# A two-layer decoder trunk on one core: earlier weight sums, a queue order, residual rows in place, a norm by column halves

## The chip, the cores and the metric

The kernel runs on one core of a Trainium2 chip. The metric is the device time of one execution in microseconds (us). The kernel before has a median of 1347.66 us over 3 runs (1346.14 to 1349.74).

## What is computed

The reference is a trunk of two post-norm layers on 512 tokens of width 1024, in float32:

```python
for l in range(DEPTH):                                   # DEPTH = 2
    proj = x @ w_in[l]
    ...
    o_a = hgrn2_mixer(hq, hf, hi, hg, lbs[l], hg_norm_w[l])      # gated linear recurrence
    o_b = nsa_mixer(nq, kc, vc, ks, vs, kw, vw, gt, ...)         # sparse attention
    mix = jnp.concatenate([o_a, o_b], axis=-1) @ w_out[l]
    x = layer_norm(ALPHA * x + mix, ln1_g[l], ln1_b[l])
    ffn = (jax.nn.silu(x @ w_ffn_gate[l]) * (x @ w_ffn_up[l])) @ w_ffn_down[l]
    x = layer_norm(ALPHA * x + ffn, ln2_g[l], ln2_b[l])
```

## The kernel before

Every product of float32 matrices is made of three TensorE matmuls on two parts: a weight or activation tile `raw` is split into a rounded part `h` (a ScalarE copy) and a rest `raw - h` (a VectorE subtraction), and `mm3` (L82 to L84) sums high x high, low x high and high x low. So each product needs one ScalarE and one VectorE instruction of its weight tile before it can run. PE is TensorE, ACT ScalarE, DVE VectorE, POOL GpSimd, SP SyncE.

A layer runs as one stream of stages, the same for both layers (times of layer 0, and of layer 1 in brackets): projections, recurrence and attention (0 to about 282 us; about 690 to 948); the out-projection with its norm, in a first half (`first_half`, contraction over the attention's first rows, 512 columns at a time) and a second half (`second_half` and the loop behind it, by quarters q of the columns), then `norm_turn` for two blocks of 256 tokens (282 to 345; 948 to 1015); gate and up (345 to 553; 1015 to 1223); the down projection (553 to 690; 1223 to 1344); the final norm.

**Gate and up** use Strassen's seven products on 2x2 blocks. `stage` loads what one unit needs: two raw tiles `a` and `d` and two sums `s1`, `s3`, each a load by SP into which POOL then issues a second DMA that adds (`accum_op`, L104 and L105). There are 20 units of seven products. `norm_rest` (L753 to L757) is the part of the norm that is left over for the residual: POOL loads the gain and shift rows, broadcast to all partitions, as one 1 MB tile `lnp` (L704), and DVE multiplies and adds on four row tiles `r`. It is hooked to a unit of this stage by number.

**Down** (`first` to `fourth`, then the loop over q with the products Q, M and N) is a Strassen scheme too. For each q = 0 to 3 a running sum of weight blocks is kept in one tile: a load, an adding DMA, split and product (`first`), a second adding DMA, split and product (`third`), a third adding DMA, split and product (`fourth`). The sums of q = 0, 1, 2 lie in the ring "f" of three buffers, that of q = 3 in `ws`. The loop behind it makes one more sum of two blocks for each q, `s3`, by a load into "f" and one adding DMA; product Q uses it. The last `fourth`, of q = 3, comes behind the products Q and M of q = 0.

What sets the order is a scheduler: it simulates the program with its own durations and gives each engine a fixed list, which the engine then works through in order. So a wait on any engine holds up all that is listed behind it, and an edit in one place reorders others. DMAs are issued by SP (plain loads) and by POOL (adding DMAs, `lnp`, and the residual loads `xr`), each in the order of its list. The weights' ring "f" is also used by `xr` (L886), by the weights of quarter 2 of the out-projection's second half (L902) and by the tile `xr2` of `norm_turn`.

Of the kernel before, what the change touches and what calls it, by code (L numbers as in the profile page):

```python
# [34 lines left out]
class Kern:  # L35
# [58 lines left out]
    def stage(self, sa, sb):  # L94

        nc = self.nc
        with self.tc.high_priority(offset=3000):
            self.turn += 1
            tag, bufs = ("wr", 2) if self.turn % 3 else ("pt", 2) if self.turn == 3 else ("f", 3)
            a = self.sb.tile([128, 1024], F32, name="wraw", tag=tag, bufs=bufs)  # L100
            s1, s3, d = (self.sb.tile([128, 512], F32, name=n, tag=t, bufs=2) for n, t in (("ws1", "st"), ("ws3", "pc"), ("wd", "wd")))
            nc.sync.dma_start(s1, sb[:, 512:])
            nc.sync.dma_start(s3, sa[:, :512])
            nc.gpsimd.dma_start(s1, sb[:, :512], accum_op=OP.add)  # L104
            nc.gpsimd.dma_start(s3, sb[:, :512], accum_op=OP.add)  # L105
            nc.sync.dma_start(a, sa)
            nc.sync.dma_start(d, sb[:, 512:])
        return a, s1, s3, d
# [619 lines left out]
    def norm_turn(self, l, which, b, rows, x, raw=None):  # L728


        nc = self.nc
        for t in (2 * b, 2 * b + 1):
            mean, rs = self.norm_stats(t)
            nb = self.small(1, "nb", tag="l")
            nc.vector.tensor_scalar(nb, mean, rs, -1.0, op0=OP.mult, op1=OP.mult)
            nc.scalar.activation(rows[t], rows[t], AF.Identity, scale=rs, bias=nb)
        for k2 in range(0, NK, 2):
            pt = self.ps("t")
            p3 = pt.rearrange("p (k t) -> p k t", t=256)
            tmp = raw(b, k2) if raw else self.m([128, 2, 256], "xt")  # L740
            for i in range(2):
                k = k2 + i
                for j in range(2):
                    nc.tensor.transpose(p3[:, i, j * 128:(j + 1) * 128], rows[2 * b + j][:, k * 128:(k + 1) * 128], self.ident)
                nc.scalar.activation(tmp[:, i], p3[:, i], AF.Identity, scale=self.lnt[:, l, 2 * which, k:k + 1],
                                     bias=self.lnt[:, l, 2 * which + 1, k:k + 1])
            xh, xl = (a[k2 // 4][:, k2 % 4:k2 % 4 + 2, b * 256:(b + 1) * 256] for a in x)
            nc.scalar.copy(xh, tmp)
            nc.vector.tensor_tensor(xl, tmp, xh.bitcast(F32), op=OP.subtract)
# [12 lines left out]
    def layer(self, l):  # L762
# [95 lines left out]
        def rblocks():  # L858
            R.extend(self.big("r") for _ in range(2))
            rows.extend(R[t // 2].rearrange("p a b -> p (a b)")[:, (t % 2) * 1024:(t % 2 + 1) * 1024] for t in range(NT))  # L860

        def quart(b, q):
# [13 lines left out]
        def first_half(c):  # L876

            def f():
                ws = [self.load_w(io["wo1"][l, c, i]) for i in range(2)]
                cs = slice(c * 512, (c + 1) * 512)  # L880
                for b in range(2):
                    pts = {t: self.ps("d") for t in (2 * b, 2 * b + 1)}
                    for i in range(2):
                        self.wide_mm(pts, ws[i], ysf, i, i == 0, i == 1)
                    xr = self.sb.tile([128, 2, 512], F32, name="xr", tag="f", bufs=3)
                    for e, (t, p) in enumerate(pts.items()):  # L886
                        nc.gpsimd.dma_start(xr[:, e], self.xres[t * 128:(t + 1) * 128, cs])
                        nc.vector.scalar_tensor_tensor(rows[t][:, cs], xr[:, e], ALPHA, p, op0=OP.mult, op1=OP.add)
            return f
# [95 lines left out]
        def up(j):  # L985
            tmp = {}

            def take(part, acc, add):
                r, c = (int(x) - 1 for x in part)
                g = hidden(j + r)  # L990
                with tc.high_priority(offset=4000):
# [14 lines left out]
        self.seven([(io[w][l, j], io[w][l, j + 1], f(j)) for j in range(2, NF, 2) for w, f in (("wg", gate), ("wu", up))], R,  # L1006
                   {3: lambda: self.norm_rest(l, 0, rows, None)})

# [24 lines left out]

        def raw_w(src, plus=None, tag=("wr", 2)):
            t = self.sb.tile([128, 1024], F32, name="wraw", tag=tag[0], bufs=tag[1])
            nc.sync.dma_start(t, src)
            if plus is not None:
                nc.gpsimd.dma_start(t, plus, accum_op=OP.add)
            return t
# [13 lines left out]
        def first(q):  # L1053

            with tc.high_priority(offset=3000):
                if q < 3:
                    s = raw_w(wd[1, 2 * q], wd[1, 2 * q + 1], ("f", 3))
                else:
                    s = self.big("ws").rearrange("p a b -> p (a b)")[:, :1024]
                    nc.sync.dma_start(s, wd[1, 2 * q])  # L1060
                    nc.gpsimd.dma_start(s, wd[1, 2 * q + 1], accum_op=OP.add)
            r11, r12, _, r22 = half[q]
# [10 lines left out]
            with tc.high_priority(offset=3000):  # L1073
                nc.gpsimd.dma_start(s, wd[0, 2 * q], accum_op=OP.add)

# [5 lines left out]
        def third(q):  # L1081
# [4 lines left out]
            with tc.high_priority(offset=3000):  # L1086
                nc.gpsimd.dma_start(sums[q], wd[0, 2 * q + 1], accum_op=OP.add)

# [34 lines left out]
        for q in range(QS):  # L1123
# [3 lines left out]
            with tc.high_priority(offset=3000):  # L1127
                s3 = raw_w(wd[0, i], wd[1, i], ("f", 3))
                p12, p22 = raw_w(wd[0, i + 1]), raw_w(wd[1, i + 1])
# [162 lines left out]
```

## Time and profile before

| what | value |
|---|---|
| median of 3 runs | 1347.66 us (1346.14 to 1349.74) |
| the profiled execution, own time | 1353.65 us |
| its span, first to last instruction | 1351.9 us |
| mean granted TensorE clock | 0.989 |
| PE, DVE, ACT, POOL busy | 97%, 75%, 55%, 14% of the span |
| DMA moved | 186.54 MB, mean 138 GB/s |

The profiled execution is 6.0 us above the median; every time in the text is from it, counted from the span's start. PE is busy nearly all the time, so what can be won or lost lies in its idle moments, some 40 us in all (the span less its busy time), and in the stretches in which its clock was granted at half.

### The profile page before, as it was taken

What the parts mean: (1) busy time and instruction counts of PE and PEld (TensorE: products, weight loads), DVE (VectorE), ACT (ScalarE), POOL (GpSimd) and SP (SyncE); (2) the same over time, 40 slices, a digit from 0 to 9 for tenths busy, and PEclk for the clock granted to TensorE, in tenths of its full rate; (3) what the DMA queues carried; (4) which work ended last, traced back from release to release, by engine and by line L of the source; (5) the groups of instructions that cost most, each with busy time, mean ns of one, the idle gap of its engine ahead of it and who ended that gap; (6) DMA issues with size and microseconds to landing.
All of it is one profiled execution on the core that took longest, in us unless ns stands there. A gap on an engine that the chain in (4) does not pass through costs nothing.

```text
span 1351.9 us, 23468 instructions
## 1 busy us (share of the span) xinstructions
PE 1311.2 (97%) x8853; PEld 1200.4 (89%) x8853; DVE 1012.4 (75%) x2021; ACT 749.6 (55%) x1495; POOL 192.5 (14%) x275
## 2 busy tenths in 40 slices
PE   8999999999999999999999999999999999999997
PEld 6988999789999999877899989987899999997776
DVE  4755798866887778967667668988559877788767
ACT  5254777844655555645452558777256555556530
POOL 1140111111011121110011100111010111111102
PEclk9999999999999999999999999999999999999999
DMA  7253212252467778586433221132515777866852
GB/s 236 79 164 102 79 56 74 84 161 76 149 167 185 189 189 197 136 223 174 152 140 116 73 92 63 63 102 71 166 29 179 178 184 180 215 158 150 213 196 79
DMA packets 67682, 186.54 MB, mean 138 GB/s; under 512 B 8175, under 2 KB 8351, under 8 KB 67056
## 3 DMA queue, kind: packets, MB, share of 16 engines
q1 hardware_dynamic: 44640, 124.73, 27.9%
q0 software_dynamic: 21920, 58.47, 21.2%
q10 hardware_dynamic: 1008, 1.84, 0.4%
q8 instruction: 69, 1.13, 0.3%
q14 instruction: 45, 0.37, 0.1%
HBM read 180.76 MB, written 7.10 MB: 139 GB/s over the span
## 4 chain that ended last, share of the span: by engine, by line
PE 59%; DVE 5%; DMA 5%; ACT 2%; issue 2%; POOL 0%; POOLq 0%; DVEq 0%; ACTq 0%
PE ps_d L83 10%; PE ps_d L82 10%; PE ps_d L84 10%; PE ps_t L84 3%; PE ps_t L82 3%; PE ps_t L83 3%; DMA wraw<-in_wd 3%; PE ps_s L82 2%; PE ps_s L83 2%; PE ps_s L84 2%; DMA ws<-in_wd 1%; PE ps_t L647 1%; DVE wlo L1019 1%; DVE hop L1019 1%; PE ps_h L390 1%
## 5 line engine op out<-in xcount | busy, mean ns | idle before, releaser
L116 ACT CAST whi<-wraw 128x512 fp32r<-128x512 f32 x160 | 98.6, 620 | 123.1 <-PE ps_d L83 93.3
L82 PE MATMUL ps_d<-xh,whi 128*128 128x256 f32 (+1 forms) x424 | 141.9, 338 | 2.0 <-ACT gates L497 1.2
L84 PE MATMUL ps_d<-xh,wlo 128*128 128x256 f32 (+1 forms) x424 | 142.6, 337 | 0.0
L83 PE MATMUL ps_d<-xl,whi 128*128 128x256 f32 (+1 forms) x424 | 141.7, 335 | 0.6 <-DVE mv L712 0.6
L117 DVE TENSOR_TENSOR wlo<-wraw,whi 128x512 fp32r<-128x512 f32 x160 | 108.9, 687 | 44.5 <-ACT whi L116 42.1
L84 PE MATMUL ps_d<-th,wlo 128*128 128x256 f32 x480 | 133.7, 284 | 2.4 <-DVE wlo L117 2.4
L83 PE MATMUL ps_d<-tl,whi 128*128 128x256 f32 x480 | 134.9, 283 | 0.0
L82 PE MATMUL ps_d<-th,whi 128*128 128x256 f32 x480 | 133.9, 283 | 0.1
L76 ACT CAST whi<-wraw 128x1024 fp32r<-128x1024 f32 (+1 forms) x68 | 70.7, 1040 | 97.0 <-PE ps_d L84 19.8
L77 DVE TENSOR_TENSOR wlo<-wraw,whi 128x1024 fp32r<-128x1024 f32 (+1 forms) x68 | 82.4, 1211 | 51.9 <-ACT whi L76 51.5
L84 PEld LDWEIGHTS ps_d<-th,wlo 128*128 128x128 f32 x480 | 91.2, 192 | 3.0 <-DVE wlo L117 3.0
L83 PEld LDWEIGHTS ps_d<-tl,whi 128*128 128x128 f32 x480 | 92.1, 192 | 0.1
L82 PEld LDWEIGHTS ps_d<-th,whi 128*128 128x128 f32 x480 | 91.4, 192 | 0.9 <-ACT su L136 0.5
L82 PEld LDWEIGHTS ps_d<-xh,whi 128*128 128x128 f32 x424 | 81.4, 193 | 9.2 <-ACT gates L497 1.3
L1019 DVE TENSOR_TENSOR wlo<-wraw,whi 128x1024 fp32r<-128x1024 f32 x50 | 60.6, 1219 | 38.3 <-ACT whi L1018 38.3
L83 PEld LDWEIGHTS ps_d<-xl,whi 128*128 128x128 f32 x424 | 81.9, 193 | 7.6 <-DVE mv L712 1.2
L84 PEld LDWEIGHTS ps_d<-xh,wlo 128*128 128x128 f32 x424 | 81.8, 193 | 7.5 <-DVE wlo L77 0.5
L83 PE MATMUL ps_d<-wlo,xh 128*128 128x256 f32 (+1 forms) x304 | 88.3, 291 | 0.0
L82 PE MATMUL ps_d<-whi,xh 128*128 128x256 f32 (+1 forms) x304 | 88.0, 291 | 0.0
L1018 ACT CAST whi<-wraw 128x1024 fp32r<-128x1024 f32 x50 | 52.3, 1051 | 64.1 <-DMA wraw<-in_wd 38.9
L84 PE MATMUL ps_d<-whi,xl 128*128 128x256 f32 (+1 forms) x304 | 87.8, 290 | 0.0
L608 ACT ACTIVATE e<-e,mn 128x128 f32<-128x128 f32 (+3 forms) x128 | 71.8, 564 | 22.1 <-DVE mn L606 21.7
(460 smaller groups left out, 4182.1 us busy)
## 6 DMA issues: line engine op xcount, KB each, us to landing
wraw<-in_wd SPq DMA_DIRECT2D x50, 512.0 KB, 4.2
wraw<-in_wf SPq DMA_DIRECT2D x31, 512.0 KB, 3.2
wraw<-in_wd POOLq DMA_DIRECT2D x26, 512.0 KB, 6.7
wraw<-in_wg SPq DMA_DIRECT2D x24, 512.0 KB, 3.9
wraw<-in_wu SPq DMA_DIRECT2D x24, 512.0 KB, 4.6
ws<-in_wg SPq DMA_DIRECT2D x40, 256.0 KB, 3.7
ws<-in_wg POOLq DMA_DIRECT2D x40, 256.0 KB, 4.7
ws<-in_wu SPq DMA_DIRECT2D x40, 256.0 KB, 3.6
```

The source lines that it names most:

```text
L76: nc.scalar.copy(h, raw[:, i:i + n])
L77: nc.vector.tensor_tensor(o, raw[:, i:i + n], h.bitcast(F32), op=OP.subtract)
L82: first = t.matmul(out, ah, bh, start=start, stop=False, **kw)
L83: t.matmul(out, ah, bl, start=False, stop=False, **kw)
L84: t.matmul(out, al, bh, start=False, stop=stop, **kw)
L116: nc.scalar.copy(h, raw)
L117: nc.vector.tensor_tensor(o, raw, h.bitcast(F32), op=OP.subtract)
L390: nc.tensor.matmul(p2[:, i], S[:, blk(i)], kq(128 * (i + 2), [[2 * w, n], [256 + w, 2], [1, w]]), start=True, stop=True)
L608: nc.scalar.activation(e, e, AF.Exp, bias=mn, scale=-1.0, accum_out=sm)
L647: nc.tensor.transpose(p[:, c:c + 128], E[qt][:, j * 128:(j + 1) * 128], self.ident)
L1018: nc.scalar.copy(dst[0], src)
L1019: nc.vector.tensor_tensor(dst[1], src, dst[0].bitcast(F32), op=OP.subtract)
```

## The change

Five edits, numbered as the prediction speaks of them (line numbers of the changed kernel are 10 to 20 higher than those of the kernel before).

1. `stage`: the raw tile `a` no longer takes every third buffer from the ring "f". So "f" is free during gate and up, and the first three sums of the down weights, which are loaded into "f", begin there.
2. `raw_w`, `add_w`: the adding DMAs of the down stage are kept in a list, and the adding DMA of each `s3` is put behind the last one issued for the running sums in POOL's list (an order, not a wait).
3. `rblocks`, `first_half`: the residual rows are loaded by four POOL DMAs of 512 KB (L872 of the changed kernel) straight into the row tiles `r`, in place of eight of 256 KB into `xr` tiles of "f" (L887 before); the update is in place (L899, before L888).
4. `norm_turn`: both tiles of a block share one aggregation and one power on POOL, the normalizing by ACT is done in 512-column halves, and for block 0 every other evacuation goes to DVE.
5. `norm_rest` of gate and up hangs on unit 6, before on unit 3.

```diff
@@ stage
-            tag, bufs = ("wr", 2) if self.turn % 3 else ("pt", 2) if self.turn == 3 else ("f", 3)
-            a = self.sb.tile([128, 1024], F32, name="wraw", tag=tag, bufs=bufs)
+            tag = "pt" if self.turn == 3 else "wr"
+            a = self.sb.tile([128, 1024], F32, name="wraw", tag=tag, bufs=2)
@@ norm_turn
-        for t in (2 * b, 2 * b + 1):
-            mean, rs = self.norm_stats(t)
...
-            nc.scalar.activation(rows[t], rows[t], AF.Identity, scale=rs, bias=nb)
+        mv = self.small(4, "mv", tag="l")
+        for j in range(2):
+            nc.vector.bn_aggr(mv[:, 2 * j:2 * j + 2], self.stats[2 * b + j].rearrange("p (a b) -> p a b", b=6))
...
+        nc.gpsimd.tensor_tensor(rs, var, self.mhalf[:, 0:2], op=OP.pow)
+        nc.vector.scalar_tensor_tensor(nb, mean, -1.0, rs, op0=OP.mult, op1=OP.mult)
+        for c in range(0, D, 512):
+            for j in range(2):
+                r = rows[2 * b + j][:, c:c + 512]
+                nc.scalar.activation(r, r, AF.Identity, scale=rs[:, j:j + 1], bias=nb[:, j:j + 1])
...
+                if b == 0 and k2 % 4:
+                    nc.vector.tensor_scalar(tmp[:, i], p3[:, i], g, c, op0=OP.mult, op1=OP.add)
+                else:
+                    nc.scalar.activation(tmp[:, i], p3[:, i], AF.Identity, scale=g, bias=c)
@@ rblocks, first_half
+            for t in range(NT):
+                nc.gpsimd.dma_start(rows[t], self.xres[t * 128:(t + 1) * 128, :])
...
-                    xr = self.sb.tile([128, 2, 512], F32, name="xr", tag="f", bufs=3)
-                    for e, (t, p) in enumerate(pts.items()):
-                        nc.gpsimd.dma_start(xr[:, e], self.xres[t * 128:(t + 1) * 128, cs])
-                        nc.vector.scalar_tensor_tensor(rows[t][:, cs], xr[:, e], ALPHA, p, op0=OP.mult, op1=OP.add)
+                    for t, p in pts.items():
+                        o = rows[t][:, cs]
+                        nc.vector.scalar_tensor_tensor(o, o, ALPHA, p, op0=OP.mult, op1=OP.add)
@@ gate and up
-                   {3: lambda: self.norm_rest(l, 0, rows, None)})
+                   {6: lambda: self.norm_rest(l, 0, rows, None)})
@@ down
+        adds = []
+        def add_w(t, plus, after=None):
+            d = nc.gpsimd.dma_start(t, plus, accum_op=OP.add)
+            if after is not None:
+                self.tc.add_manual_dep(d.ins, after.ins.name, mybir.DependencyInfo(
+                    mybir.DependencyClass.NoSync, mybir.DependencyReason.DATA), reason="queue order")
+            adds.append(d)
...
-                s3 = raw_w(wd[0, i], wd[1, i], ("f", 3))
+                s3 = raw_w(wd[0, i], wd[1, i], ("f", 3), adds[-1])
```

What the scheduler makes of it, at the three places of which the prediction speaks:

POOL's list, from the last norm of layer 0's out-projection into gate and up. Before (`lnp_4124` is the gain and shift tile):

```order
L104 DMA ws1_3998<-in_wg 128x512
L714 TENSOR_TENSOR rstd_3481<-mv_3478,mhalf_122 128x1
L704 DMA lnp_4124<-in_ln 128x2048
L105 DMA ws3_3999<-in_wg 128x512
L104 DMA ws1_4135<-in_wu 128x512
```

and with the change (`wraw_6312`, `wraw_6340` and `wraw_6386` are the down sums of q = 0, 1, 2, L1048 their adding DMA, `lnp_4487` the gain and shift tile):

```order
L104 DMA ws1_3982<-in_wg 128x512
L1048 DMA wraw_6312<-in_wd 128x1024
L1048 DMA wraw_6340<-in_wd 128x1024
L704 DMA lnp_4487<-in_ln 128x2048
L1048 DMA wraw_6386<-in_wd 128x1024
L105 DMA ws3_3983<-in_wg 128x512
L104 DMA ws1_4109<-in_wu 128x512
```

Two adding DMAs of 512 KB now stand ahead of `lnp` and one behind it. On SP the three loads of these sums stand where three raw tiles `a` of later units stood (L106). DVE's list still has the four multiplications by `lnp` together near the start of the stage, in spite of edit 5; with the change:

```order
L117 TENSOR_TENSOR wlo_3757<-wraw_3855,whi_3756 128x512
L117 TENSOR_TENSOR wlo_3757<-wd_3763,whi_3756 128x512
L766 TENSOR_TENSOR r_2790<-r_2790,lnp_4487 128x1024 x2
L766 TENSOR_TENSOR r_2791<-r_2791,lnp_4487 128x1024 x2
L162 TENSOR_TENSOR wraw_3855<-wraw_3855 128x512
L117 TENSOR_TENSOR wlo_3755<-ws3_3857,whi_3754 128x512
L767 TENSOR_TENSOR r_2790<-r_2790,lnp_4487 128x1024
```

The split of `wd` stood behind the four multiplications before, and stands ahead of them now.

POOL's list at the end of layer 0's down sums. Before (L1074 and L1087 are the second and third adding DMA of a running sum, L1038 that of an `s3` or of a first sum; `wraw_6658` is the `s3` of q = 0, `ws_6470` the running sum of q = 3):

```order
L1087 DMA wraw_6328<-in_wd 128x1024
L1074 DMA ws_6470<-in_wd 128x1024
L1087 DMA wraw_6356<-in_wd 128x1024
L1038 DMA wraw_6658<-in_wd 128x1024
L1087 DMA wraw_6402<-in_wd 128x1024
L1038 DMA wraw_6747<-in_wd 128x1024
L1087 DMA ws_6470<-in_wd 128x1024
```

and with the change (all are L1048; `wraw_6642` is the `s3` of q = 0, `ws_6454` the running sum of q = 3):

```order
L1048 DMA wraw_6312<-in_wd 128x1024
L1048 DMA ws_6454<-in_wd 128x1024
L1048 DMA wraw_6340<-in_wd 128x1024
L1048 DMA wraw_6386<-in_wd 128x1024
L1048 DMA ws_6454<-in_wd 128x1024
L1048 DMA wraw_6642<-in_wd 128x1024
L1048 DMA wraw_6731<-in_wd 128x1024
```

The third adding DMA of `ws` no longer stands behind that of the second `s3`; the first `s3` now stands behind it.

ACT's list at the end of layer 0's attention, with the change (`wraw_3169` is the weight tile of quarter 2 of the out-projection's second half, `pth` a part of the attention):

```order
L651 CAST pth_3126<-ps_t_3122 128x384
L76 CAST wx_3171<-wraw_3169 128x1024
L651 CAST pth_3135<-ps_t_3131 128x384
```

Before, the two `pth` casts stood next to each other and that of quarter 2's weights came some 10 us later. On PE the 48 matmuls of quarter 2 over rows that are there already move with it, from behind the first half to ahead of its end.

## Rows read from the trace of the kernel before

**Rows 1.** The page, first part: each engine's busy us, share of the span and number of instructions.

```profile
PE 1311.2 (97%) x8853; PEld 1200.4 (89%) x8853; DVE 1012.4 (75%) x2021; ACT 749.6 (55%) x1495; POOL 192.5 (14%) x275
```

**Rows 2.** Waits of PE over the whole span: who waited for whom, us in total, times, longest us.

```profile
PE ps_t L82 <- ACT whi L1018: 5.7, 3, 2.2
...
PE ps_d L82 <- DVE r L888: 2.9, 2, 2.3
PE ps_t L744 <- ACT xraw L745: 2.6, 2, 1.3
```

**Rows 3.** Windows of 25 us, the starts of gate and up in layers 0 and 1: length, then busy us of PE, PEld, DVE, ACT and POOL, the granted clock, the DMA share and GB/s.

```profile
350.00:375.00 25.00, 22.67 (x186) 22.05 (x185) 24.89 (x34) 14.91 (x29) 3.16 (x4) 1.00 0.63 192
...
1025.00:1050.00 25.00, 22.27 (x179) 21.49 (x178) 25.00 (x39) 13.33 (x28) 3.42 (x4) 1.00 0.61 178
```

**Rows 4.** Windows of 3.4 us, PE alone: length, busy us, the granted clock, the DMA share and GB/s.

```profile
326.80:330.20 3.40, 3.23 (x16) 0.50 0.27 82
610.10:613.50 3.40, 2.98 (x7) 0.50 1.06 211
...
965.10:968.50 3.40, 3.40 (x10) 0.50 0.83 270
```

**Rows 5.** Timeline of DVE and of PE at the start of gate and up, layer 0: start, us, engine, line, operation, and in brackets the idle time before it and what ended it. L948 frees the first buffer of "f".

```profile
346.42 1.22 DVE L948 SCALAR_TENSOR_TENSOR xraw<-xr,xr 128x1024 f32<-128x1024 f32 x1
...
361.05 4.62 DVE L756 TENSOR_TENSOR r<-r,lnp 128x1024 f32<-128x1024 f32 x4
365.59 0.68 DVE L162 TENSOR_TENSOR wraw<-wraw 128x512 f32<-128x512 f32 x1
...
367.42 0.39 PE L82 MATMUL ps_t<-xh,whi 128*128 128x256 f32 x1 [0.87 <-ACT whi L116]
```

**Rows 6.** Timeline of SP and POOL there: when the first two raw tiles into "f" and `lnp` were issued.

```profile
347.85 0.33 SPq L106 DMA_DIRECT2D wraw<-in_wu  x1
348.92 0.33 SPq L106 DMA_DIRECT2D wraw<-in_wg  x1
...
354.29 0.60 POOL L704 DMA_DIRECT2D lnp<-in_ln  x1 [22.72 <-DVE tl L951]
```

**Rows 7.** One line's instructions: L106 from 347 to 351 us, its three loads of 512 KB, us from issue to landing.

```profile
DMA to landing us min/median/max: 3.5/3.8/4.7
```

**Rows 8.** One line's instructions: L704, the four loads of `lnp` (1 MB) of the kernel, us from issue to landing.

```profile
DMA to landing us min/median/max: 4.8/5.2/6.9
```

**Rows 9.** Timeline of DVE at the same place in layer 1.

```profile
1014.99 1.22 DVE L948 SCALAR_TENSOR_TENSOR xraw<-xr,xr 128x1024 f32<-128x1024 f32 x1
...
1031.89 2.35 DVE L756 TENSOR_TENSOR r<-r,lnp 128x1024 f32<-128x1024 f32 x2
```

**Rows 10.** One line's instructions: L1038, 14 adding DMAs of 512 KB, us from issue to landing. L1038 is the first of a pair or alone, but for the last, at 1279.55 us, which took the 7.2.

```profile
DMA to landing us min/median/max: 5.1/5.4/7.2
```

**Rows 11.** Timeline of POOL in the down stages of layer 0 and layer 1: the adding DMA of the second `s3`, and what it waited for.

```profile
598.09 0.85 POOL L1038 DMA_DIRECT2D wraw<-in_wd  x1 [10.09 <-DMA wraw<-in_wd]
...
1267.98 0.85 POOL L1038 DMA_DIRECT2D wraw<-in_wd  x1 [8.51 <-DMA wraw<-in_wd]
```

**Rows 12.** The chain that ended last, in order of time, its pieces of the third adding DMA of `ws`: start, us from issue to landing.

```profile
598.63 10.04 DMA ws<-in_wd
...
1268.52 9.21 DMA ws<-in_wd
```

**Rows 13.** Timeline of DVE, the second split of `ws` in each layer.

```profile
592.19 1.23 DVE L1019 TENSOR_TENSOR wlo<-ws,whi 128x1024 fp32r<-128x1024 f32 x1 [0.89 <-ACT whi L1018]
...
1264.14 1.22 DVE L1019 TENSOR_TENSOR wlo<-ws,whi 128x1024 fp32r<-128x1024 f32 x1 [0.89 <-ACT whi L1018]
```

**Rows 14.** Timeline of ACT in layer 0, behind the cast of the first `s3`: two copies (`dv`) and the cast for product M.

```profile
600.98 1.06 ACT L1100 COPY dv<-ps_d 128x512 f32<-128x512 f32 x2
601.93 1.05 ACT L1018 CAST whi<-wraw 128x1024 fp32r<-128x1024 f32 x1
```

**Rows 15.** Timeline of PE, the start of product Q of q = 0 and the gaps behind it, layer 0 and then layer 1.

```profile
601.85 0.39 PE L82 MATMUL ps_d<-whi,hop 128*128 128x512 f32 x1
...
609.86 1.05 PE L82 MATMUL ps_t<-whi,hop 128*128 128x512 f32 x2 [2.02 <-ACT whi L1018]
611.33 1.22 PE L82 MATMUL ps_s<-whi,hop 128*128 128x512 f32 x2 [0.42 <-ACT whi L1018]
...
1273.73 0.39 PE L82 MATMUL ps_d<-whi,hop 128*128 128x512 f32 x1
...
1280.39 0.73 PE L82 MATMUL ps_s<-whi,hop 128*128 128x512 f32 x2 [0.61 <-ACT whi L1018]
```

**Rows 16.** Timeline of PE in the out-projection, the first matmul behind the wait for the residual update, layer 0 and layer 1.

```profile
297.23 0.50 PE L82 MATMUL ps_d<-whi,y 128*128 128x512 f32 x1 [0.61 <-DVE r L888]
...
964.27 0.50 PE L82 MATMUL ps_d<-whi,y 128*128 128x512 f32 x1 [2.27 <-DVE r L888]
```

**Rows 17.** One line's instructions: L58 from 275 to 276 us, the load of quarter 2's weights, issued at 275.1, and its us to landing.

```profile
L58 SPq DMA_DIRECT2D wraw<-in_wo x1: 328/328/328, 275.1 to 275.1; - x1
...
DMA to landing us min/median/max: 4.6/4.6/4.6
```

**Rows 18.** The same for the load of another quarter's weights at 233.7 us, beside six loads of residual rows by POOL.

```profile
DMA to landing us min/median/max: 6.0/6.0/6.0
```

**Rows 19.** Timeline of ACT at the end of the attention, layer 0.

```profile
280.11 0.48 ACT L651 CAST pth<-ps_t 128x384 fp32r<-128x384 f32 x1 [0.32 <-DVE y L460]
```

More of the change, by code (lines that the diff above doesn't have):

```diff
@@ L731, in norm_turn @@
         nc = self.nc
-        for t in (2 * b, 2 * b + 1):
-            mean, rs = self.norm_stats(t)
-            nb = self.small(1, "nb", tag="l")
-            nc.vector.tensor_scalar(nb, mean, rs, -1.0, op0=OP.mult, op1=OP.mult)
-            nc.scalar.activation(rows[t], rows[t], AF.Identity, scale=rs, bias=nb)
+        mv = self.small(4, "mv", tag="l")
+        for j in range(2):
+            nc.vector.bn_aggr(mv[:, 2 * j:2 * j + 2], self.stats[2 * b + j].rearrange("p (a b) -> p a b", b=6))
+        mean, var = (mv.rearrange("p (t a) -> p a t", a=2)[:, a] for a in range(2))
+        nc.vector.tensor_scalar(var, var, 1e-5, None, op0=OP.add)
+        rs, nb = (self.small(2, name, tag="l") for name in ("rstd", "nb"))
+        nc.gpsimd.tensor_tensor(rs, var, self.mhalf[:, 0:2], op=OP.pow)
[4 more added lines that the diff above has]
+                nc.scalar.activation(r, r, AF.Identity, scale=rs[:, j:j + 1], bias=nb[:, j:j + 1])
         for k2 in range(0, NK, 2):
@@ L744, in norm_turn @@
                     nc.tensor.transpose(p3[:, i, j * 128:(j + 1) * 128], rows[2 * b + j][:, k * 128:(k + 1) * 128], self.ident)
-                nc.scalar.activation(tmp[:, i], p3[:, i], AF.Identity, scale=self.lnt[:, l, 2 * which, k:k + 1],
-                                     bias=self.lnt[:, l, 2 * which + 1, k:k + 1])
+                g, c = (self.lnt[:, l, 2 * which + e, k:k + 1] for e in range(2))
+                if b == 0 and k2 % 4:
+                    nc.vector.tensor_scalar(tmp[:, i], p3[:, i], g, c, op0=OP.mult, op1=OP.add)
+                else:
+                    nc.scalar.activation(tmp[:, i], p3[:, i], AF.Identity, scale=g, bias=c)
             xh, xl = (a[k2 // 4][:, k2 % 4:k2 % 4 + 2, b * 256:(b + 1) * 256] for a in x)
@@ L1032, in split_w, with raw_w @@
             return w
-        def raw_w(src, plus=None, tag=("wr", 2)):
+        adds = []
[5 more added lines that the diff above has]
+            adds.append(d)
+        def raw_w(src, plus=None, tag=("wr", 2), after=None):
             t = self.sb.tile([128, 1024], F32, name="wraw", tag=tag[0], bufs=tag[1])
@@ L1037, in raw_w @@
             if plus is not None:
-                nc.gpsimd.dma_start(t, plus, accum_op=OP.add)
+                add_w(t, plus, after)
             return t
@@ L1060, in first @@
                     nc.sync.dma_start(s, wd[1, 2 * q])
-                    nc.gpsimd.dma_start(s, wd[1, 2 * q + 1], accum_op=OP.add)
+                    add_w(s, wd[1, 2 * q + 1])
             r11, r12, _, r22 = half[q]
@@ L1073, in first @@
             with tc.high_priority(offset=3000):
-                nc.gpsimd.dma_start(s, wd[0, 2 * q], accum_op=OP.add)
+                add_w(s, wd[0, 2 * q])
         def second(q):
@@ L1086, in third @@
             with tc.high_priority(offset=3000):
-                nc.gpsimd.dma_start(sums[q], wd[0, 2 * q + 1], accum_op=OP.add)
+                add_w(sums[q], wd[0, 2 * q + 1])
         def fourth(q):
```

## The prediction

> **What bounds the kernel now.** Read the busy times first: PE works 97% of the span, the next engine 75% [rows 1]. A faster engine beside PE therefore gains nothing by itself; only PE's own gaps and its clock can move the end. Then read the waits of PE [rows 2]: apart from the attention, which the change leaves alone, they are waits for splits of down weights (ps_t, 5.7 us), for the residual update (2.9 us) and for the transposes' evacuation (2.6 us). Third, windows: in some stretches of 3.4 us the granted clock is 0.50, the lower level of 1.2 GHz [rows 4]. The one at 610.1 us follows the gap of 2.02 us, the one at 965.1 us the gap of 2.27 us [rows 15, 16]; half the rate for 3.4 us costs 1.7 us, so a gap of 2 us or more is priced with 1.7 us on top. Last, the 25 us at the start of gate and up: DVE is busy for 24.89 and 25.00 of 25 us [rows 3]. There DVE is the bound and PE waits for it.
>
> **The sums at the start of gate and up (edits 1 and 5).** The three loads take the place of three raw tiles into the same ring, so they go out when those did: 347.85, 348.92 us and one more [rows 6], and land in 3.5 to 4.7 us [rows 7]. New are three adding DMAs of 512 KB at that moment. POOL's list has two of them ahead of `lnp`. Each goes out about half a microsecond after its load has landed: 351.9 and 353.2 us; `lnp` behind them at 353.8 us, about as before (354.29). What is different is what lies ahead in the queue. An adding DMA alone lands in 5.1 to 5.4 us [rows 10]. One issued 0.54 us behind another lands in 10.0 and 9.2 us [rows 11, 12], that is 4 to 5 us after the first; the shortest such time is 7.2 us, some 3 us after the first [rows 10]. So POOL's DMAs get through one after the other. The first add lands at 351.9 + 5.2 = 357.1 us, the second 3 to 5 us later, at 360 to 362 us, and `lnp` behind it. Its 1 MB takes 4.8 to 5.2 us alone [rows 8], 512 KB 3.5 us [rows 7]: the second 512 KB cost some 1.5 us, the whole about 3 us of moving data. `lnp` lands at 361.1 + 3 = 364.1 us; bounds are 353.8 + 5.1 = 358.9 us (nothing in front matters) and 367 us (behind loads of SP that also start at 358 us).
>
> The Trainium skill ("DMA: Bandwidth & Descriptors", Queues, rings and completion order) says that completion is not first-in first-out per issuing engine; if that let `lnp` pass the adds, it would land at the lower bound and this term would be nothing. The same section says that each DMA engine consumes a ring's descriptors in order, and the pairs above go with that.
>
> DVE reached its first use of `lnp` at 361.05 us [rows 5]. The list has the same number of splits ahead of it as before, so it will get there at about the same time and wait 3.0 us, with all splits of gate and up queued behind. Those four instructions take 4.62 us, then comes L162, 0.6 us, then ACT's cast of its result, 0.6 us, then PE. Before, that chain ended PE's gap of 0.87 us at 367.42 us [rows 5], with DVE without any slack [rows 3]; so 3.0 us more for DVE are a gap of about 3.9 us, 3.0 us more. That `wd`'s split stands ahead now gives some of it back: I take **2.7 us**. A gap above 2 us brings the clock term, **1.7 us**. In layer 1 the ring frees at 1014.99 + 1.22 = 1016.2 us, against 347.6 us in layer 0 [rows 5, 9]; `lnp` lands 16.5 us behind that, at 1032.7 us, and DVE's four instructions end at 1037.3 us in place of 1034.2 us [rows 9], less the 0.7 us split that now stands ahead: **2.3 us**, and again **1.7 us**. Sum **+8.4 us**; bounds 0 and +14.
>
> Edit 1 itself, the tile `a` in a ring of two, I cost at nothing: a load lands in under 5 us [rows 7], and a unit of seven products lasts about 10 us (20 units in 208 us), with the load issued at the end of the last-but-one unit. If that cover went, each unit would wait some microseconds and the change would be slower by tens of us; nothing suggests it. Edit 5 moves nothing by itself: the four instructions stand at the same place in DVE's list.
>
> **POOL's order in down (edit 2).** The third add of `ws` was issued at 598.63 us [rows 12], behind an `s3` add that waited for its load [rows 11], though `ws` had been split by 592.19 + 1.23 = 593.4 us [rows 13]. Now it goes at 593.5 us, lands before 600 us, and the gaps of 2.02 and 0.42 us with their clock term of 1.7 us, together 4.1 us, go away [rows 4, 15]. But the first `s3` now stands behind it: issued at 594.05 us, second of a pair, it lands 7.2 to 10.2 us later; I take 8.5, between the shortest and the usual 9 to 10, since fewer loads run beside it: 602.6 us. Behind it stand its cast (1.05 us), a copy (0.53) and M's cast (1.05) [rows 14], and PE wants M's first matmul right after Q's first two: PE can go on at 605.2 us and would be there at 601.85 + 0.46 = 602.3 us [rows 15]. That is a gap of 2.9 us, plus 1.7 us of clock: 4.6 us for 4.1 us, **+0.5 us**. In layer 1 the split ends at 1264.14 + 1.22 = 1265.4 us [rows 13], the `s3` add goes at 1266.0, lands at 1274.5, and M can start at 1277.1 us against 1273.73 + 0.46 = 1274.2 us: the same 2.9 + 1.7 us, for a gap of only 0.61 us [rows 15]: **+4.0 us**. Sum **+4.5 us**. With a landing of 5.1 us there is no gap at all and the term is −4.7 us; with 10.2 us it is about +8.
>
> **Residual rows and the out-projection (edit 3).** The ring "f" is free of residual tiles, quarter 2's weights are split some 10 us earlier, and the load of quarter 3 no longer waits for that. The gaps of 0.61 and 2.27 us [rows 16] and the clock behind the second [rows 4] go: −4.6 us. The price is on ACT: the cast of quarter 2's weights now stands ahead of a cast of the attention that ran at 280.11 us [rows 19]. Its load was issued at 275.1 us and landed in 4.6 us [rows 17], at 279.7 us; with the four residual loads (issued from 266 us on) beside it, up to 6.0 us [rows 18], at 281.1 us. PE takes the tile's high part at about 280.8 us (now 280.8 to 282.2) and its rest, 1.2 us of DVE later, after half a microsecond of other work: a gap of 0.7 to 2.1 us; I take 1.0 us, nearer the uncrowded row, because 2 MB from 266 us on are nearly through by 275 us. Twice 1.0: net **−2.6 us**; bounds −4.6 and +2.
>
> **The norm (edit 4)** I cost at **0**. For block 0 the chain lies under matmuls of block 1. For block 1 PE's wait for the evacuation (1.3 us twice [rows 2], with half a clock behind it [rows 4]) stays, since the second half of the columns stands last on ACT as before. If halves free the transposes earlier, both go, −6 us; if the twelve transposes that now stand in a row wait for two evacuation buffers, it is +2 us.
>
> **The sum** is 8.4 + 4.5 − 2.6 + 0 = +10.3 us: 1353.65 becomes 1364.0 us for a profiled execution, which lay 6.0 us above the median; the median 1347.66 becomes **1358 us**. The forecast is slower, with a range of its own of 1351 to 1366 us.
>
> **The rivals.**
> *Both DMAs are in time* (faster). `lnp` lands before 361 us and the first `s3` within 5.5 us of issue. It decides at those two times. For it: alone, both would (5.1 us). Against: pairs took 9 to 10 us. The first term is 0, the second −4.7, with −2.6: −7.3 us, 1340 us; with the norm's gaps gone as well, 1335 us. Chance 0.30.
> *Only `lnp` is late*: the `s3` add finds the queue empty enough. 8.4 − 4.7 − 2.6 = +1.1 us, 1349 us. Chance 0.12.
> *Only `s3` is late*: `lnp`, a plain load, moves past adding DMAs, or DVE gets to it later than before. The Trainium skill's sentence on completion order, above, would make it so. 4.5 − 2.6 = +1.9 us, 1350 us. Chance 0.13.
> *The change does not do what it says* is true of edit 5 already, and is in the sum.
>
> **How the numbers follow.** The forecast has 0.45. A measurement of this kernel can tell about 0.3%, 4 us, from no change. Faster: the first rival, and the second and third where the norm also gains: 0.34. Within 4 us: most of these two, and the forecast's low edge: 0.20. Slower: 0.46. The range runs from the first rival's 1340 us, a little below it, up to the forecast's upper part: 1339 to 1364 us.
>
> **What would show it.** Right: DVE idle for 2 to 5 us before the first multiplication by `lnp` in both layers, released by the DMA; a PE gap of 3 to 4 us at about 366 and 1035 us with the clock at 0.50 behind it; Q's and M's casts of q = 0 released by the `s3` add, with a PE gap at about 602 us (after shifts) and its like in layer 1; no gap at the residual update; a short PE wait for the `wx` cast near 281 us. Wrong: `lnp` landing in 5 to 6 us as before, or the `s3` add doing so; a new wait on a raw tile `a`.

## The result and the profile after

The changed kernel takes 1364.12 us (median of 4 runs, 1360.04 to 1365.37) against 1348.7 us for the kernel before beside it: ratio 1.0108, 95% interval 1.0078 to 1.0139. It is slower, by more than the 0.3% that can be told apart. The profiled execution took 1364.38 us (span 1362.6 us), 10.7 us more than that of the kernel before; the prediction's sum was +10.3.

Waits of PE over the whole span, changed kernel (who waited for whom, us in total, times, longest us):

```profile
PE ps_t L82 <- ACT whi L116: 8.2, 2, 4.5
PE ps_d L82 <- ACT whi L1029: 6.0, 4, 2.7
...
PE ps_t L82 <- ACT whi L1029: 3.3, 2, 3.0
PE ps_h L457 <- DVE hy L454: 2.2, 6, 0.9
...
PE ps_t L751 <- DVE xraw L754: 1.9, 3, 0.8
PE ps_t L751 <- ACT xraw L756: 1.7, 4, 0.7
```

Against [rows 2]: the wait for the residual update is gone, and two new ones lead: one for the split of gate and up (L116, once in each layer) and one of product Q for the cast of its weight sum (L1029). The timelines of the engines show what is behind the first. POOL at the start of gate and up, layer 0:

```profile
351.19 0.86 POOL L1048 DMA_DIRECT2D wraw<-in_wd  x1 [20.88 <-PE ps_d L84]
352.44 0.86 POOL L1048 DMA_DIRECT2D wraw<-in_wd  x1 [0.39 <-DVE tl L962]
352.98 0.88 POOL L704 DMA_DIRECT2D lnp<-in_ln  x1
353.91 0.85 POOL L1048 DMA_DIRECT2D wraw<-in_wd  x1
```

`lnp` goes out 1.3 us earlier than before [rows 6], but behind two adding DMAs. L704's instructions, who waited for them and their landing; the lower figure is the one load at 353.0 us alone:

```profile
  DVE r L766: 7.9, 3
...
DMA to landing us min/median/max: 5.6/8.2/11.5
...
DMA to landing us min/median/max: 11.5/11.5/11.5
```

Before it was 4.8 to 6.9 us [rows 8]. So DVE stands still in both layers, 4.17 and 3.35 us, and PE behind it. DVE, then PE, both layers (in brackets the idle time and what ended it):

```profile
364.49 4.63 DVE L766 TENSOR_TENSOR r<-r,lnp 128x1024 f32<-128x1024 f32 x4 [4.17 <-DMA lnp<-in_ln]
...
1040.10 4.63 DVE L766 TENSOR_TENSOR r<-r,lnp 128x1024 f32<-128x1024 f32 x4 [3.35 <-DMA lnp<-in_ln]
```

```profile
370.43 0.58 PE L82 MATMUL ps_t<-xh,whi 128*128 128x256 f32 x1 [4.51 <-ACT whi L116]
...
612.60 1.28 PE L82 MATMUL ps_d<-whi,hop 128*128 128x512 f32 x2 [2.58 <-ACT whi L1029]
...
1046.04 0.58 PE L82 MATMUL ps_t<-xh,whi 128*128 128x256 f32 x1 [3.68 <-ACT whi L116]
...
1284.14 1.28 PE L82 MATMUL ps_d<-whi,hop 128*128 128x512 f32 x2 [2.70 <-ACT whi L1029]
```

The 0.87 us of [rows 5] has become 4.51 us. The gaps at 612.60 and 1284.14 are product Q's. Behind each of the four the clock is at half; windows of PE alone, length, busy us, granted clock, DMA share, GB/s:

```profile
369.70:373.10 3.40, 1.59 (x4) 0.50 0.76 160
373.10:376.50 3.40, 3.19 (x15) 0.50 0.19 34
612.05:615.45 3.40, 2.70 (x5) 0.50 0.67 99
615.45:618.85 3.40, 3.40 (x9) 0.50 0.89 220
1045.55:1048.95 3.40, 1.61 (x5) 0.50 0.88 181
1048.95:1052.35 3.40, 3.40 (x16) 0.50 0.33 49
1284.50:1287.90 3.40, 3.25 (x8) 0.50 0.49 82
```

Three of the stretches last 6.8 us, twice as long as those of [rows 4]; the last ends after 3.4 us. What they cost is half of the time that PE is busy in them, since it can lose nothing while it stands idle: some 2.4, 3.1, 2.5 and 1.6 us. Last, the chain that ended last, in order of time (start, us), and POOL's list at the first of its pieces: the three late DMAs lie on the critical chain, and the `s3` add of q = 0 stands second, behind the third add of `ws`.

```profile
602.33 9.10 DMA wraw<-in_wd
...
1029.31 10.77 DMA lnp<-in_ln
...
1273.98 8.98 DMA wraw<-in_wd
```

```profile
601.79 0.85 POOL L1048 DMA_DIRECT2D ws<-in_wd  x1 [7.11 <-DVE wlo L1030]
602.33 2.08 POOL L1048 DMA_DIRECT2D wraw<-in_wd  x2
```

Where the 10.7 us came from, by the time of the first matmul of each stage in both traces of PE (after less before, us):

| stretch | layer 0 | layer 1 |
|---|---|---|
| to the first transpose for the out-projection (L457, at 245 us in layer 0 before) | -2.0 | +0.1 |
| out-projection and norm, to gate and up's first matmul (at 326 us) | +1.6 | -2.2 |
| gate and up | +5.2 | +3.7 |
| down | +4.6 | -0.4 |

The change touches nothing in the first stretch of layer 0: there the profiled execution of before had a half-clock stretch at 12.8 us, which that of after has not (windows of before, then of after). In twelve of the thirteen other profiles of this case that stretch is 0.3 to 2.0 us shorter than in that of before.

```profile
12.80:16.20 3.40, 3.40 (x9) 0.50 1.06 394
...
12.80:16.20 3.40, 3.40 (x15) 1.00 1.05 392
```

The norm of the second block still runs beside the first matmuls of gate and up. To see the wait for `lnp` alone, count PE's matmuls (8853 in both): the one that ran at 352.0 us now runs 0.9 us earlier, the one of 375.0 us runs 4.9 us later, and the shift stays at 4.9 us to the end of the stage. In layer 1 it grows from 6.5 us (at 1023.1 us) to 11.1 us (at 1060.1 us). So the starts of gate and up cost 5.8 and 4.6 us.

### The profile page after: what moved, and what is told of

The parts are those of the page before. It is cut to its first block, busy times and chain, and to the rows that moved or that the text cites. A ratio compares the mean times of both kernels' runs of the same rounds, so it can differ in the third digit from the quotient of the medians.

```text
span 1362.6 us, 23443 instructions
## 1 busy us (share of the span) xinstructions
PE 1315.0 (97%) x8853; PEld 1204.5 (88%) x8853; DVE 1015.9 (75%) x2021; ACT 749.9 (55%) x1495; POOL 182.5 (13%) x261
## 4 chain that ended last, share of the span: by engine, by line
PE 83%; issue 5%; DMA 4%; DVE 4%; ACT 2%; POOL 1%; POOLq 0%; DVEq 0%; ACTq 0%
PE ps_d L82 15%; PE ps_d L83 15%; PE ps_d L84 15%; PE ps_s L82 3%; PE ps_s L83 3%; PE ps_t L84 3%; PE ps_s L84 3%; PE ps_t L82 3%; PE ps_t L83 3%; PE ps_t L647 2%; PE ps_h L390 1%; DMA wraw<-in_wd 1%; PE ps_o L658 1%; PE ps_o L657 1%; PE ps_s L519 1%
## 5 line engine op out<-in xcount | busy, mean ns | idle before, releaser
L116 ACT CAST whi<-wraw 128x512 fp32r<-128x512 f32 x160 | 98.4, 620 | 131.8 <-PE ps_d L83 93.9
L1029 ACT CAST whi<-wraw 128x1024 fp32r<-128x1024 f32 x50 | 52.4, 1052 | 72.6 <-DMA wraw<-in_wd 39.7
```

The lines of the kernel that those rows point to most:

```text
L116: nc.scalar.copy(h, raw)
L1029: nc.scalar.copy(dst[0], src)
```

## The experiments

The theory: two DMAs became late, `lnp` behind the early adds and the first `s3` behind `ws`'s last add, and the rest of the change is worth little. The rivals: the early sums cost by their traffic or buffers wherever `lnp` stands; the queue order as such is at fault; the norm or the residual rows cost what was put down to the DMAs. Every ratio below is to the kernel before on the same chip; a difference of two ratios carries both intervals, some 0.003 to 0.004 either way.

**`lnp` ahead of the early adds.** An order in POOL's list, no wait:

```diff
-                    s = raw_w(wd[1, 2 * q], wd[1, 2 * q + 1], ("f", 3))
+                    s = raw_w(wd[1, 2 * q], wd[1, 2 * q + 1], ("f", 3), self.ln_dma)
```

> The changed kernel with one order added: the three adding DMAs of the early down sums stand behind the load of lnp in POOL's list (an order, no wait), so lnp is first. Theory (lnp is late because POOL's DMAs are served one after the other): lnp lands in 5 to 6 us again, at 358 to 359.5 us, before DVE gets to it; DVE's wait for it (4.2 and 3.5 us) is gone, PE's gaps of 4.51 and 3.68 us shrink to about 1 us each and the clock stays full there; 6.6 + 6.1 us are won over the change, ratio to the kernel before 0.997 to 1.003. Rival (the early sums take DMA bandwidth wherever they stand in the list, 2 MB loaded and 1.5 MB added in ten us): lnp lands only 1 to 2 us earlier than with the change, and the ratio stays at 1.006 to 1.010. Second rival (DVE is the bound there, so PE waits elsewhere for the same time): lnp is in time, but new PE gaps of the same sum appear by 390 us, ratio 1.007 to 1.011.

1.0039 (1.0017 to 1.006): 0.0069 less than the change, or 9.3 us, a little short of the range expected. DVE no longer waits for `lnp`, which lands in 4.7 to 6.6 us. PE at the same place, and the windows around it:

```profile
366.97 0.39 PE L82 MATMUL ps_t<-xh,whi 128*128 128x256 f32 x1 [0.87 <-ACT whi L116]
368.90 0.39 PE L82 MATMUL ps_t<-th,whi 128*128 128x256 f32 x1 [1.43 <-DVE h_at L989]
```

```profile
366.50:369.90 3.40, 1.50 (x9) 1.00 1.06 337
370.00:373.40 3.40, 3.40 (x18) 0.51 0.72 160
373.40:376.80 3.40, 3.40 (x30) 1.00 0.82 128
```

The 0.87 us of the kernel before is back. Two gaps of 2.30 us together stand here, where the kernel before had 2.33 us in three and kept the full clock [rows 3]. Its second and third:

```profile
369.00 0.38 PE L84 MATMUL ps_d<-th,wlo 128*128 128x256 f32 x1 [0.84 <-DVE wlo L117]
...
371.07 0.38 PE L84 MATMUL ps_t<-th,wlo 128*128 128x256 f32 x1 [0.62 <-DVE wlo L117]
```

Here 3.4 us at half clock follow, 1.7 us lost. This kernel also still has Q's gaps (2.54 and 2.71 us); freeing Q's first add as well takes 0.0028 of the 0.0039 away (both repairs, below).

**The ring as before, so no early sums.**

```diff
-            tag = "pt" if self.turn == 3 else "wr"
-            a = self.sb.tile([128, 1024], F32, name="wraw", tag=tag, bufs=2)
+            tag, bufs = ("wr", 2) if self.turn % 3 else ("pt", 2) if self.turn == 3 else ("f", 3)
+            a = self.sb.tile([128, 1024], F32, name="wraw", tag=tag, bufs=bufs)
```

> The changed kernel with edit 1 alone undone: every third raw tile takes a buffer of the ring f again, so the first three down sums are loaded and added late in gate and up, as before the change; all else stays. Theory: the same as with lnp first, since what costs is only what stands ahead of lnp: lnp in 5 to 6 us, ratio 0.997 to 1.003. If early sums are worth something in themselves, this kernel is slower than the one with lnp first by over 0.3%; the theory expects no difference between the two beyond 0.3%. Rival (bandwidth): this one is faster than the one with lnp first by 0.4 to 0.8%.

1.0039 (1.0025 to 1.0053), the same as with `lnp` ahead, with the same two gaps. So, as far as the two intervals can tell (some 0.003), early sums cost nothing and gain nothing but by where `lnp` stands; the ring of two for `a` is free.

**One add ahead of `lnp` in place of two.**

```diff
-                    s = raw_w(wd[1, 2 * q], wd[1, 2 * q + 1], ("f", 3))
+                    s = raw_w(wd[1, 2 * q], wd[1, 2 * q + 1], ("f", 3), self.ln_dma if q else None)
```

> The changed kernel with one adding DMA ahead of the load lnp in GpSimd's list in place of two: a dose test. Theory: lnp waits for the adds ahead of it one by one, so it lands at about 360.2 to 361.5 us in layer 0 (364.5 with two ahead, about 357 to 359 with none), VectorE waits for it 1 us at most, the landing time of the group is 7 to 8.5 us, and the ratio is 1.004 to 1.006 beside 1.011 with two. Rival: the delay is bytes in flight of all transfers, whatever the list: lnp lands late as before, VectorE waits 3 to 4 us, ratio about 1.010.

1.0093 (1.0061 to 1.0124): above the range of the theory and next to the rival's figure. The trace has to decide. POOL's issues, then, for each of these four DMAs in this order, its us to landing (from each line's own instructions):

```profile
350.73 0.86 POOL L1048 DMA_DIRECT2D wraw<-in_wd  x1 [19.78 <-PE ps_d L84]
352.08 0.56 POOL L704 DMA_DIRECT2D lnp<-in_ln  x1 [0.50 <-DMA wraw<-in_wd]
352.62 0.90 POOL L1048 DMA_DIRECT2D wraw<-in_wd  x1
353.72 0.84 POOL L1048 DMA_DIRECT2D wraw<-in_wd  x1 [0.20 <-issue]
```

```profile
DMA to landing us min/median/max: 6.6/6.6/6.6
...
DMA to landing us min/median/max: 9.6/9.6/9.6
...
DMA to landing us min/median/max: 11.9/11.9/11.9
...
DMA to landing us min/median/max: 14.0/14.0/14.0
```

They land at 357.4, 361.7, 364.5 and 367.7 us, in the order of issue and some 3 to 4 us apart. `lnp` has moved up by 2.8 us and the add now behind it has taken its place at 364.5: the list decides, as the theory says. The price does not follow the dose. DVE came to `lnp` earlier too, waited 2.25 us, and PE had two gaps:

```profile
368.24 0.38 PE L82 MATMUL ps_t<-xh,whi 128*128 128x256 f32 x1 [2.59 <-ACT whi L116]
370.80 0.58 PE L82 MATMUL ps_t<-th,whi 128*128 128x256 f32 x1 [2.05 <-DVE h_at L989]
```

Together 4.64 us, against 5.81 in three gaps with two adds ahead and 2.30 with none, and the half clock lasted 6.8 us as with two. So one add costs most of what two cost.

**The queue order of the `s3` adds undone.**

```diff
-                s3 = raw_w(wd[0, i], wd[1, i], ("f", 3), adds[-1])
+                s3 = raw_w(wd[0, i], wd[1, i], ("f", 3), None)
```

> The changed kernel with edit 2 undone: no order for the adding DMA of s3. The scheduler puts the first s3 ahead of the third adding DMA of q = 2, and the second s3 ahead of that of ws, as in the kernel before. Theory: PE's gaps at product Q of q = 0 (2.58 us with 6.8 us of half clock in layer 0, 2.70 with 3.4 us in layer 1) go, and in their place come the gaps before the last fourth (about 2.0 + 0.4 us with 3.4 us of half clock in layer 0, 0.6 + 0.6 us in layer 1): 1.9 + 3.2 us won over the change, ratio 1.005 to 1.009. Rival (the gap at Q comes from the loads of SP beside it, not from POOL's order): the gap at Q stays and the ratio is within 0.2% of the change's 1.0108.

1.009 (1.0069 to 1.0112), the end of the range expected. Q's gaps of 2.58 and 2.70 us are gone, but the third add of `ws` is late again, 10.12 us from 602.93 us, as in [rows 12], and PE waits 0.96 and 0.73 us behind it. The order as a whole costs 0.0018, within what the two intervals leave open; in this profile the half clock behind `lnp`'s gap in layer 1 lasted 10.2 us, longer than in that of the changed kernel.

**The first `s3` alone free to go ahead of `ws`'s last add.**

```diff
+        last_add = adds[-1]
...
-                s3 = raw_w(wd[0, i], wd[1, i], ("f", 3), adds[-1])
+                s3 = raw_w(wd[0, i], wd[1, i], ("f", 3), last_add if q else None)
```

> The changed kernel with edit 2 for q = 1, 2, 3 alone: the first s3 is free to go ahead (it stands ahead of the third adding DMA of q = 2), the second s3 stays behind the third one of ws. Theory: neither wait is left, no PE gap over 1 us at product Q or before the last fourth in either layer: 2.58 + 3.4 + 2.70 + 1.7 = 10.4 us won over the change, ratio 1.001 to 1.005. Rival (some add is late whatever the order, since 512 KB take 4 to 5 us each in POOL's queue and five are wanted in 20 us): the gap moves to the third product of q = 2 or to the last fourth, with 2 us or more, and the ratio is 1.006 to 1.010.

1.0065 (1.005 to 1.0081): 0.0043 less than the change, 5.8 us; the interval just reaches the range expected. POOL's list in layer 0 now has the first `s3` with the pair ahead of `ws`:

```profile
590.49 1.72 POOL L1048 DMA_DIRECT2D wraw<-in_wd  x2 [8.14 <-DMA wraw<-in_wd]
597.78 0.85 POOL L1048 DMA_DIRECT2D ws<-in_wd  x1 [5.57 <-DVE wlo L1030]
```

Q's gaps are gone in both layers; a later product of layer 0 waits 1.48 us. The cost of the queue order was thus in its first `s3`; for the pairs behind it the order does no harm.

**Both repairs together.**

> The changed kernel with both repairs: the load lnp ahead of the three early adds, and the first adding DMA of the fourth sums free to go ahead of those of the last sum. Theory: the two losses are apart and add, so their repairs do too: lnp_ahead gave 1.0039, and the free first add takes 0.0043 (1.0108 less 1.0065) off it: ratio 0.998 to 1.002. Rival: the second repair moves the wait to the last sum, whose adds then come late: ratio 1.003 or more.

1.0011 (0.9991 to 1.0032), as the theory had it: the two losses add (0.0069 and 0.0043 against 0.0097 together, within the intervals), and without them the changed kernel cannot be told from the kernel before.

**The norm and the residual rows in the kernel before**: both, then each alone (edits 3 and 4, as in the diff of the change).

> The kernel before with two parts of the change alone: the residual rows loaded in place ahead of the out-projection, and the norm of two row blocks at once by column halves. Early sums, ring and queue order stay as before. Theory: these two parts gain, most of it in layer 1, where the changed kernel lost the out-projection's wait of 2.27 us and its half-clock stretch (1.7 us): the stages say about 3.1 us less, ratio 0.9975 to 0.9995. Rival: the gain at that place was chance of that one profile and the parts are worth nothing: ratio 1.000.

> The kernel before with one part of the change: the residual rows loaded in place ahead of the out-projection. Theory: layer 1's wait of 2.27 us and its half-clock stretch go (about 3 us between the first out-projection transpose and gate and up), layer 0 keeps its time, and the start of gate and up stays as in the kernel before: ratio 0.9965 to 0.9985. Rival: what went there was a stall of one profiled execution only, or comes back as a wait for the out-projection's own transposes: ratio 0.9995 to 1.001.

> The kernel before with another part alone: the norm of two row blocks at once by column halves. Theory: it is this part that makes the kernel with both parts no faster. The norm's end moves VectorE's queue against the matmuls, so that the split that TensorE needs stands behind two scaling operations in place of one: gaps of 0.87 and 1.43 us with a half-clock stretch of 3.4 us behind them in each layer, in place of three short gaps without one. Ratio 1.002 to 1.005. Rival: the norm costs nothing, and the start of gate and up differs by chance from run to run: ratio 0.999 to 1.001, gaps of three as before.

1.0015 (0.9993 to 1.0037), 1.0003 (0.9985 to 1.002) and 0.999 (0.9974 to 1.0007). My theory falls in all three: neither the gain of the residual rows nor a cost of the norm is seen. What edit 3 removes is real in the traces. Waits of PE for the residual update, the kernel with the norm alone:

```profile
PE ps_d L82 <- DVE r L898: 4.1, 2, 2.8
```

and none in any of the kernels with edit 3. But the kernels with it have half-clock stretches of 3.4 us at the start of gate and up in both layers, where the kernel before has none, and PE waits more for `hy`, whose transposes feed the out-projection (L457: 0.9 us before, 2.2 after). Wherever `lnp` was in time and DVE's eight operations on it stood in one clump, gaps of 1.6 to 2.3 us in two or three pieces were left there; such a stretch followed them in 11 of 12 cases (six profiles, two layers), in the one profile of the kernel before in neither layer. What decides it is not settled, and so it stays open whether edit 3's gain of some 3 us is taken back there or was never there on average; the last two kernels below bear on it.

**The scaling operations spread.** The two repairs, and DVE's eight operations on `lnp` one to each of units 3 to 10, each ordered behind the last split:

```diff
-            nc.vector.tensor_tensor(o, raw, h.bitcast(F32), op=OP.subtract)
+            self.last_split = nc.vector.tensor_tensor(o, raw, h.bitcast(F32), op=OP.subtract)
...
+    def norm_part(self, l, rows, n):
...
+        r, h = rows[n // 2], n % 2
+        d = self.nc.vector.tensor_tensor(r, r, self.lnp[:, h * 1024:(h + 1) * 1024], op=OP.add if h else OP.mult)
+        self.tc.add_manual_dep(d.ins, self.last_split.ins.name, mybir.DependencyInfo(
...
-                   {6: lambda: self.norm_rest(l, 0, rows, None)})
+                   {n + 3: lambda n=n: self.norm_part(l, rows, n) for n in range(8)})
```

> Both repairs, and the eight VectorE operations that scale and shift the rows after the norm, which stand in one clump behind gate and up's sixth unit, spread one to each of units 3 to 10, each behind the last split that VectorE has issued by then. Theory: the clump of some 8 us is what still stops TensorE there (0.87 and 1.43 us and a half-clock stretch of 3.4 us, in each layer); without it these go, some 3 to 4 us per layer: ratio 0.993 to 0.998. Rival: VectorE's work in this stage is the bound whatever its order, and the gaps come back in later units: ratio 0.999 to 1.002.

0.9957 (0.994 to 0.9975): faster than both kernels. Windows of 25 us at the starts of gate and up, columns as in [rows 3]:

```profile
350.00:375.00 25.00, 24.96 (x208) 24.76 (x207) 19.07 (x32) 16.60 (x33) 6.26 (x8) 1.00 1.02 275
1015.00:1040.00 25.00, 24.84 (x207) 24.64 (x206) 18.70 (x32) 15.75 (x33) 6.54 (x8) 1.00 0.97 256
```

PE is busy for 24.96 of 25 us, before for 22.67; DVE, which was full, has 6 us to spare. In neither layer is a PE gap above 0.3 us left in the stage. So it was the clump, not DVE's work in the stage, that stopped PE there, and the rival falls.

**Spread without the change, and with the residual rows alone.**

> The kernel before with the eight scaling operations of the rows spread one to each of units 3 to 10, and nothing of the change. Theory: the clump costs the kernel before 2.3 us in each layer (its gaps of 0.87, 0.84 and 0.62, and of 1.10 and 1.17 us), so their spreading gains 4 to 5 us without any part of the change: ratio 0.995 to 0.998. Rival: the spreading gains only together with the early sums, which take load from VectorE later: ratio 0.999 to 1.002.

> The kernel before with the residual rows in place and the scaling operations spread: the two parts that the profiles price as gains, without the early sums, the queue order and the norm by halves. Theory: the gains add, some 3 and 4 to 5 us: ratio 0.992 to 0.996, below the change with both repairs and the spreading (0.9957). Rival: the residual rows in place are worth nothing by themselves: ratio as with the spreading alone, 0.995 to 0.998.

0.9967 (0.9949 to 0.9985) and 0.9942 (0.9925 to 0.9959). The spreading gains without any part of the change. The residual rows add 0.0025 to it, 3.4 us, as their theory says, now that no clump stands behind them. The two intervals overlap, but both kernels ran on one chip beside each other, and 8 of the 11 times with the residual rows lie below the lowest of the 12 without (1343.18 us). The profiles show where: with the spreading alone PE waits for the residual update, 1.76 and 3.07 us, with 3.4 us at half clock behind each, and with edit 3 not at all.

```profile
PE ps_d L82 <- DVE r L897: 4.8, 2, 3.1
```

By its ratio the last kernel is the fastest of all (1342.49 us), without early sums, queue order or norm by halves.

## Why the prediction was right, and where its sizes were off

**`lnp` (+8.4).** Right in each step up to PE's gaps. Its landing was forecast at 364.1 us and came at 364.5 (352.98 + 11.48). In layer 1 it came at 1040.1, which is 1032.7 to 1033.6 without the kernel's own shift there (7.4 us at gate and up's first matmul, 6.5 by count); 1032.7 was forecast. DVE waited 4.17 and 3.35 us against 3.0, since it was there before 361.05 us, at 360.3. Two sizes were off. PE's gaps grew by 3.5 us in layer 0 (5.81 us for 2.33) and by 2.3 in layer 1 (4.98 for 2.65), where 2.7 and 2.3 were forecast. The clock behind them cost 2.4 and 2.5 us and not 1.7: it was at half for 6.8 us, in which PE was busy for 4.8 and 5.0. That makes 5.9 and 4.8 us; by count the starts of gate and up cost 5.8 and 4.6. By the ratios the repair gives 9.3 us, with some 5 us either way, though the repaired kernel keeps 3.4 us at half clock there in each layer, which the kernel before has not.

The clock's price, 1.7 us behind a gap of 2 us or more, did not fit the prediction's own rows either: the stretch at 326.8 us [rows 4] stands behind a gap of 1.30 us [rows 2].

The sentence that completion is not first-in first-out per issuing engine (the Trainium skill, "DMA: Bandwidth & Descriptors", Queues, rings and completion order) stands there in a paragraph on the queues of SP and ACT; the rival "only `s3` is late" carried it over to POOL's. That was not borne out here: of the 180 DMAs that POOL issued in the changed kernel 97 went out before the one ahead of them had landed, and none landed before it, nor did one overtake with one add ahead. The same section's other sentence, that descriptors of one ring are consumed in order, agrees with the landings in order, 3 to 4 us apart.

**`s3` (+4.5).** Right. It was issued second of a pair and landed in 9.10 and 8.98 us (8.5 forecast). PE stood for 2.58 and 2.70 us (2.9 forecast) at Q's first matmul; the forecast had counted to M's, two matmuls on. With the clock behind them (3.1 and 1.6 us) against the gaps before, 2.02 and 0.42 us with 1.5, and 0.61 without, that is +1.7 and +3.7 us, +5.4; freeing the first `s3` gives 5.8 by the ratios. The rest of the down stages' shifts, +2.9 and -4.1, are gaps at a third add of a first sum (3.02 us in place of 1.39 at 584 us, 0.31 in place of 2.25 at 1259) and the half clock behind the two long ones; such gaps lay between 0.3 and 3.8 us in the kernels run here, with and without the change.

**Residual rows (-2.6) and norm (0).** The gaps of [rows 16] went, and the wait for the cast of quarter 2's weights near 281 us, priced at 1.0 us twice, did not come: the residual loads were through by 272.7 us and that load landed in 3.5 us (273.2 to 276.7), not in 4.6 to 6.0. In its place PE waited 0.88 and 0.44 us for `hy`, ahead of its transposes. With the norm the stretch came out at +1.6 and -2.2 us, -0.6 in all; up to the points counted above, where the second block's norm is through, at -2.1. By the ratio the two edits together are worth +0.0015 (-0.0007 to +0.0037), some +2.0 us, so -2.6 us is not confirmed. The norm's waits for the evacuation became two of 0.80 and 0.66 us in place of one of 1.30: nothing, as forecast. The early sums' ring and the hook were nothing too.

**The steps that failed** are the term of the residual rows and the last step of the sum: +10.3 us, taken on one profiled execution, was laid on the median. By the ratios the two late DMAs are worth 9.3 and 5.8 us and edits 3 and 4 some +2.0, where the sum had 8.4, 4.5 and -2.6; so the gain that did not come is the largest miss, though each of these figures carries some 3 to 5 us either way. The median rose by some 15 us, and 1364.12 us stands 0.1 us above the end of the range given (1339 to 1364), where 1358 was the forecast. That the profiled executions differ by +10.7 us, as the sum did, is in part luck: between them the terms came to 10.4, 5.4 and -2.1 us, 13.7 in all, and some -3 us came from stretches for which the sum had no term, -1.9 ahead of the out-projections and -1.2 at the third adds. The profiled execution of before contained such losses and lay 6.0 us above its median; that of after lay 0.3 us above its own.

## What to carry to other kernels

A DMA on GpSimd's queue is as late as all that its list puts ahead of it: before work is moved earlier, list what it now stands ahead of, and whether an engine without slack waits for that. Here one entry of the list, put ahead of three adds, was worth 9 us, with some 5 us either way. And where an engine is full for 25 us and has room behind it, spread its clump: that gained 0.3% without any of the five edits.

## What the runs showed of the hardware

Half-clock stretches behind gaps of much the same length were of different lengths: 3.4 us behind Q's 2.70 us, 6.8 us behind its 2.58, 6.8 us behind 3.68 and 4.51 us. Nor does the length of a gap tell whether one follows: in the kernel before, the attention of both layers has the same gap, and behind 1.67 us (at 244.9 us) the clock stayed full, while behind 1.68 us (at 908.7 us) it was at half from 910.5 to 913.9 us. So 1.7 us is not the price of every gap above 2 us, and a shorter gap is not free.

Four DMAs issued on POOL within 3 us with one add ahead of `lnp`, 512 KB added, 1 MB loaded, and twice 512 KB added, landed 4.3, 2.8 and 3.2 us apart, in order of issue; in the changed kernel `lnp` landed 3.5 and 3.6 us behind the add ahead of it. So a load of 1 MB took 3.5 to 4.3 us of the queue, an add of 512 KB about 3 us, though one alone takes 5 to 6 us from issue to landing.
